# Attention's transposes as pairs of 64x128 blocks on two banks, and the first memory attention's scores on four quarters of the array

## The chip, the cores and the metric

The kernel runs on one core of a Trainium2 chip. The metric is device time in microseconds, the median of three runs. A core has a matrix engine (TensorE, in the profile PE, its weight loads PEld), a vector engine (VectorE, DVE), a scalar engine (ScalarE, ACT), GpSimd (POOL) and a queue engine for transfers (SyncE, SP). TensorE writes only to PSUM, which has eight banks; ScalarE or VectorE copies a result from there to SBUF.

## The reference

Two layers of a trunk over 512 positions of width 1024. Layer 0 mixes with RWKV-7 (12 heads of 64), layer 1 with chunked attention (12 heads, own chunk and 8 chunks before it). Beside each mixer runs a memory attention of four heads over 256 memory tokens. The part that the change touches:

```python
def memory_attention(q_mem, mem_n, w_mem_kv):
    ...
    s = jnp.einsum('bshd,bmhd->bhsm', q, k).astype(jnp.float32) * HEAD_DIM ** -0.5
    p = jax.nn.softmax(s, axis=-1).astype(v.dtype)
    return jnp.einsum('bhsm,bmhd->bshd', p, v).reshape(bsz, seq, D_MEMQ)

def chunk_attention(q, k_pad, v_pad, bias):
    ...
        s = jnp.einsum('bhqd,bhkd->bhqk', qc, kc).astype(jnp.float32) * scale + bias
        ...
        p = jax.nn.softmax(s, axis=-1).astype(vc.dtype)
        return jnp.einsum('bhqk,bhkd->bhqd', p, vc)

for layer in range(DEPTH):
    mix = rwkv7_time_mix(...) or chunk_attention(...)
    mo = memory_attention(q_mem, mem_n, w_mem_kv[layer])
    x = x + jnp.concatenate([mix, mo], axis=-1) @ w_out[layer]
    x = x + conv_glu(rms_norm(x, ln2[layer]), ...)
```

## The kernel before

The program is one stream of instructions for each engine, written by Python generators. `weave` takes several generators, each with a cost, and always continues the one that has done the least share of its own cost; a `yield n` says that about n ns of TensorE work were written. So the costs of the generators set the order in which TensorE sees the work of different stages. Each engine runs its own stream in order and waits at semaphores. The weights of the dense projections come in as f32, are split into a high and a low part (`whi`, `wlo`) and are multiplied in three products (`dense`, lines 241, 242 and 245), always as 128x128 weights with 512 moving columns.

Heads come in pairs, one on partitions 0 to 63, the other on 64 to 127 (`HS[0]`, `HS[1]`). An attention computes its scores with queries on the partitions, does a softmax along the row (a maximum on VectorE, the exponential with its sum on ScalarE, a reciprocal and a scaling on VectorE), transposes the probabilities on TensorE in blocks of 128x128 against the constant `ident`, copies them from PSUM with ScalarE, and multiplies them by the values.

`mem_attention` does this for the memory tokens. `rows` is scores and softmax for one head and two halves `q2` of the positions, `turn` the transposes (line 360) and copies (line 363) of a head, two banks one after the other, and `values` the product with the values (line 370) for both heads `hh` of a pair `f`. It is used twice. In layer 0 (`mA`) the scores are plain f32 matmuls of 64 rows (`score_a`, line 1590), and the generator is woven with `back` for the fifth head pair, `front` and `back` for the sixth, and `out_ahead`, the first products of the output projection. `back` turns RWKV's chunk products into outputs: it begins with small products (lines 1410, 1418, 1424, 1434, 1445, 1453, 1462) and ends with a recurrence of eight steps (lines 1467, 1472 on TensorE, 1468 on VectorE). In layer 1 (`memB`) the scores are split products of 128 rows.

`attention(i, T)` is the chunked attention of head pair `i`. For each quarter `qt` of the positions and each head, `rows` (lines 1788 and 1789, then 1793 to 1797) computes `qt + 1` blocks of probabilities, and `turn` transposes them (line 1803) three row steps later (`LAG`) and copies them (line 1805) into `ptT`. Line 1817 multiplies all four quarters by the values. Six of these generators and `memB` form one chain, woven with the projections of queries, keys and values. Attention has six PSUM banks for the small products (`pss`), the stage of layer 0 four.

Lines 1300 to 1326 in `front` already use the array in parts: line 1314 transposes 64x128 blocks of the two heads in turn into two banks, and lines 1324 and 1326 multiply 64x64 weights on all four quarters.

## Time and profile before

| | |
|---|---|
| median of three runs | 1292.26 us (1291.12 to 1293.33) |
| profiled execution, span from the first to the last instruction | 1292.6 us; the page gives no other time of it |
| TensorE, matmuls | 1260.9 us busy, 10420 records |
| VectorE | 1031.7 us busy |
| ScalarE | 846.4 us busy |
| transposes of the chunked attention (line 1803) | 120, 21.1 us busy, between 759.8 and 910.5 us |
| transposes of the second memory attention (line 360) | 32, 5.1 us busy, between 803.7 and 823.1 us |
| first memory attention, first to last score or transpose | 310.6 to 345.2 us |

The page lists for every engine the time in which it was busy. A matmul in plain f32 leaves two records in the trace, a transpose and a matmul of split operands one. Matmuls overlap: one is counted from its start to the end of its tail, so what one costs is seen from the distance to the start of the next. A shape such as "64*128 64x64" reads: weights on 64 rows and 128 columns of the array, 64 rows by 64 moving columns. A row of the timeline gives the start, the length of the merged row, the engine, the line, and what was written from what.

### The profile page before, as it was taken

Reading aid. Unit: us, or ns where it says so; the run is one execution under the profiler, and the core shown is the slowest. Engines: PE = TensorE matmul, PEld = TensorE weight load, DVE = VectorE, ACT = ScalarE, POOL = GpSimd, SP = SyncE. Lnnn points to the kernel's source line nnn. Section 1 sums busy time; section 2 is a strip of 40 time slices with the busy share of each in tenths; the row PEclk is TensorE's granted clock in tenths of the full one; section 3 lists DMA queues with packets and bytes.
Section 4 is the critical chain, followed back from the end, with each engine's and each line's share of the span. In section 5 each row is a group of like instructions: output and inputs, shape, how many; then the busy total and the mean of one; then the engine's idle time right before and its main releaser. Section 6 shows DMA issues by size and latency. Waiting matters only on the chain.

```text
span 1292.6 us, 26432 instructions
## 1 busy us (share of the span) xinstructions
PE 1260.9 (98%) x10420; PEld 1083.1 (84%) x10420; DVE 1031.7 (80%) x1956; ACT 846.4 (65%) x1398; POOL 152.7 (12%) x182
## 2 busy tenths in 40 slices
PE   9999999999999999999999999999999999999997
PEld 7887777777789999998888878787789999998886
DVE  7867677765688999998876876658889999998684
ACT  6566767856476777776554676757757777765662
POOL 1000000000001222320220000000002222211200
PEclk9999999999999999999999999999999999999999
DMA  5364444453055988996984322234429989978951
GB/s 204 110 174 106 100 96 89 92 109 96 30 166 126 212 198 198 206 208 172 274 185 122 118 87 82 76 104 123 130 61 212 197 193 211 208 161 262 233 149 66
DMA packets 95581, 192.14 MB, mean 149 GB/s; under 512 B 22112, under 2 KB 30432, under 8 KB 95456
## 3 DMA queue, kind: packets, MB, share of 16 engines
q1 hardware_dynamic: 68592, 129.14, 31.9%
q0 software_dynamic: 26864, 61.31, 27.3%
q8 instruction: 82, 1.34, 0.4%
q14 instruction: 43, 0.35, 0.1%
HBM read 174.20 MB, written 6.29 MB: 140 GB/s over the span
## 4 chain that ended last, share of the span: by engine, by line
PE 62%; DVE 15%; ACT 8%; DMA 8%; issue 6%; SPq 0%; POOL 0%; ACTq 0%; DVEq 0%; POOLq 0%
PE psf L434 8%; PE psf L698 7%; PE psd L245 6%; PE psd L241 5%; PE psd L242 5%; DMA wlv<-in_ffn_in_dram 4%; PE psf L436 4%; PE psf L703 4%; PE psd L698 3%; ACT whi L499 2%; DMA wraw<-in_ffn_in_dram 2%; PE psd L703 2%; DVE raw L486 1%; PE pss L1817 1%; DVE wlo L504 1%
## 5 line engine op out<-in xcount | busy, mean ns | idle before, releaser
L499 ACT CAST whi<-raw 128x1024 fp32r<-128x1024 f32 (+1 forms) x168 | 153.3, 942 | 62.3 <-PE psf L434 29.5
L434 PE MATMUL psf<-th,whi 128*128 128x256 f32 x672 | 161.4, 278 | 2.5 <-ACT tmp L553 1.9
L434 PE MATMUL psf<-tl,whi 128*128 128x256 f32 x672 | 161.1, 276 | 0.0
L195 ACT CAST whi<-wraw 128x1024 fp32r<-128x1024 f32 x84 | 87.6, 1048 | 78.3 <-PE psd L242 37.4
L434 PEld LDWEIGHTS psf<-th,whi 128*128 128x128 f32 x672 | 125.8, 188 | 3.9 <-ACT tmp L553 2.9
L434 PEld LDWEIGHTS psf<-tl,whi 128*128 128x128 f32 x672 | 126.0, 188 | 0.0
L504 DVE TENSOR_TENSOR wlo<-raw,whi 128x1024 fp32r<-128x1024 f32 (+1 forms) x108 | 109.3, 1012 | 9.1 <-ACT whi L499 8.9
L241 PE MATMUL psd<-r1h,whi 128*128 128x512 f32 x264 | 107.4, 408 | 0.0
L242 PE MATMUL psd<-r1l,whi 128*128 128x512 f32 x264 | 105.0, 398 | 0.0
L203 DVE TENSOR_TENSOR wlo<-wraw,whi 128x1024 fp32r<-128x1024 f32 x65 | 79.2, 1219 | 22.3 <-ACT whi L195 20.4
L688 ACT CAST whi<-raw 128x1024 fp32r<-128x1024 f32 (+1 forms) x52 | 49.6, 954 | 59.9 <-PE psf L698 33.1
L689 DVE TENSOR_TENSOR wlo<-raw,whi 128x1024 fp32r<-128x1024 f32 (+1 forms) x52 | 56.5, 1097 | 38.9 <-ACT whi L688 31.5
L436 PE MATMUL psf<-th,wlo 128*128 128x256 f32 x504 | 78.0, 276 | 0.0
L245 PE MATMUL psd<-r1h,wlo 128*128 128x512 f32 x264 | 74.3, 403 | 0.6 <-DMA wlo<-in_ffn_in_dram 0.4
L471 POOL DMA_DIRECT2D wlv<-in_ffn_in_dram x40 | 60.7, 1516 | 59.5 <-DVE tmp L572 59.1
L436 PEld LDWEIGHTS psf<-th,wlo 128*128 128x128 f32 x504 | 66.8, 188 | 0.0
L434 PE MATMUL psf<-r2h,whi 128*128 128x256 f32 x252 | 60.9, 278 | 0.7 <-ACT whi L499 0.7
L434 PE MATMUL psf<-r1h,whi 128*128 128x256 f32 x252 | 60.7, 277 | 0.7 <-ACT whi L499 0.7
L434 PE MATMUL psf<-r2l,whi 128*128 128x256 f32 x252 | 60.7, 277 | 0.0
L434 PE MATMUL psf<-r1l,whi 128*128 128x256 f32 x252 | 60.6, 277 | 0.0
L241 PEld LDWEIGHTS psd<-r1h,whi 128*128 128x128 f32 x264 | 49.6, 188 | 12.0 <-issue 2.1
L525 ACT ACTIVATE tmp<-tmp,vec 128x512 f32<-128x512 f32 x44 | 36.0, 817 | 33.3 <-DVE tmp L512 33.3
(611 smaller groups left out, 3576.8 us busy)
## 6 DMA issues: line engine op xcount, KB each, us to landing
raw<-in_ffn_in_dram SPq DMA_DIRECT2D x42, 512.0 KB, 5.2
raw<-in_ffn_in_dram SPq DMA_DIRECT2D x84, 256.0 KB, 5.5
wlv<-in_ffn_in_dram POOLq DMA_DIRECT2D x40, 512.0 KB, 8.6
raw<-in_ffn_out_dram SPq DMA_DIRECT2D x30, 512.0 KB, 6.2
raw<-in_ffn_out_dram POOLq DMA_DIRECT2D x24, 512.0 KB, 8.4
wraw<-in_wA_dram SPq DMA_DIRECT2D x20, 512.0 KB, 4.1
wraw<-in_w_out_dram SPq DMA_DIRECT2D x16, 512.0 KB, 4.1
wraw<-in_ffn_outp_dram SPq DMA_DIRECT2D x16, 512.0 KB, 4.5
```

The costliest lines, as they stand in the source:

```text
L195: high = lambda: pin(SC.copy(hi[:, :n], raw))
L203: pin(V.tensor_tensor(lo[:, :n], raw, hi[:, :n], op=ALU.subtract))
L241: PE.matmul(ps, wh[:, j * P:(j + 1) * P], ah, start=start and n == 0, stop=False)
L242: dense_at[0] = PE.matmul(ps, wh[:, j * P:(j + 1) * P], al, start=False, stop=False)
L245: dense_at[0] = PE.matmul(ps, wl[:, j * P:(j + 1) * P], act(k)[0], start=False, stop=stop and n == len(ks) - 1)
L434: PE.matmul(ps, wh[:, o + k * P:o + k * P + P], x[k][n], start=k == n == 0, stop=False)
L436: PE.matmul(ps, wl[:, ol + k * P:ol + k * P + P], x[k][0], start=False, stop=k == 3)
L471: GP.dma_start(self.low[:].rearrange("p (a s) -> p a s", a=2), self.second, accum_op=ALU.add)
L499: keep(SC.copy(hi[:, :n], self.pair(what) if n > S else self.raw[:, what]))
L504: keep(V.tensor_tensor(lo[:, :n], self.pair(what) if n > S else self.raw[:, what], hi[:, :n], op=ALU.subtract))
L698: PE.matmul(ps[:], a[:, k0 + i, ts], hi[:, i * S:i * S + S], start=bool(first) and (first is True or t in first) and a is act[0] and i == ...
L703: PE.matmul(ps[:], act[0][:, k0 + i, ts], lo[:, i * S:i * S + S], start=False, stop=bool(last) and t in last and i == n - 1)
```

## The change

It does four things.

1. `turned` replaces each transpose of a 128x128 block by two of its halves, 64 rows by 128 columns each, against the 64x64 identity `i64`. Rows 0 to 63 go to one bank, rows 64 to 127 to another, 64 columns each. So a `turn` holds two banks at once, and each bank has every second group of 64 positions.
2. In the chunked attention `turn` takes both heads of a quarter, after `rows` of both heads of the quarter behind it; the transposes of the heads are separated by a yield, and four copies follow, by head and bank, where there were two of double width. The cost of a block falls from 0.85 x 128 = 109 to 68.
3. In `mem_attention`, `turn` has two copies by bank in layer 1 (of the same 512 elements), and four of 256 in layer 0.
4. In layer 0 the scores of both heads are written together, each as two matmuls of 64x64 weights, in the order of `QUADS` over the four quarters of the array, and both heads go through the softmax half by half. The order is now all scores and softmaxes of a pair, then the transposes of both its heads. The costs given to `weave` fall (860 to 450, 430 to 270).

```diff
+    def turned(ps, at, src, of):
+        for i in range(2):
+            PE.transpose(ps[i][:, at:at + 64], src[i * 64:i * 64 + 64, of:of + P], C("i64")[i * 64:i * 64 + 64])
...
+        def scores(f, hhs, q2):
+            ps = {hh: ps_s() for hh in hhs}
+            for qq in range(2):
+                score({hh: ps[hh][:, qq * 256:(qq + 1) * 256] for hh in hhs}, f,
+                      slice((q2 * 2 + qq) * P, (q2 * 2 + qq + 1) * P))
+            return ps
...
         def turn(f, hh):
+            ps = [ps_s() for _ in range(2)]
             for kt in range(2):
-                ps = ps_s()
                 for qt in range(4):
-                    o = (qt % 2) * 256 + kt * P
-                    PE.transpose(ps[:, qt * P:(qt + 1) * P], prs[f, hh, qt // 2][:, o:o + P], C("ident"))
-                yield 430
-                t_ = pts[f, hh, kt] = pt_tile(f, hh, kt)
-                SC.copy(t_, ps[:])
+                    turned(ps, (kt * 4 + qt) * 64, prs[f, hh, qt // 2], (qt % 2) * 256 + kt * P)
+                yield 270
+            ts = [pt_tile(f, hh, kt) for kt in range(2)]
+            for kt in range(2):
+                pts[f, hh, kt] = ts[kt]
+            for i in range(2):
+                pt_copy(f, hh, i, ps[i][:].rearrange("p (k q c) -> p k q c", k=2, c=64))
...
+        if l == 0:
+            for f in range(2):
+                yield from rows(f, (0, 1))
+                if f:
                     yield from values(0)
-        yield from turn(1, 1)
+                yield from turn(f, 0)
+                yield from turn(f, 1)
...
+    QUADS = ((0, 0), (1, 1), (0, 1), (1, 0))
...
-    def score_a(ps, f, hh, qc):
-        PE.matmul(ps, qmA[f][HS[hh], qc], kmT0[HS[hh], f], start=True, stop=True)
+    def score_a(ps, f, qc):
+        for hh, n in QUADS:
+            PE.matmul(ps[hh][HS[n]], qmA[f][HS[hh], qc.start + n * 64:qc.start + n * 64 + 64], kmT0[HS[hh], f], start=True, stop=True)
+
+    def pt_copy_a(f, hh, i, half):
+        for kt in range(2):
+            SC.copy(ptA[hh * 2 + kt].rearrange("p (q c) -> p q c", c=P)[:, :, i * 64:i * 64 + 64], half[:, kt])
...
-            def turn(hh, qt):
-                n = (qt + 1) * P
-                pst_ = ps_s()
-                for kt in range(qt + 1):
-                    PE.transpose(pst_[:, kt * P:(kt + 1) * P], sbs[hh, qt][:, kt * P:(kt + 1) * P], C("ident"))
-                yield n * 0.85
-                SC.copy(pts[hh][:, 0:qt + 1, qt * P:(qt + 1) * P], pst_[:, :n].rearrange("p (a b) -> p a b", b=P))
...
+            def turn(qt):
+                n = qt + 1
+                ps = [ps_s() for _ in range(2)]
+                for hh in range(2):
+                    for kt in range(n):
+                        turned(ps, (hh * n + kt) * 64, sbs[hh, qt], kt * P)
+                    yield n * 68
+                for hh in range(2):
+                    for i in range(2):
+                        SC.copy(pts[hh][:, 0:n, qt * P + i * 64:qt * P + i * 64 + 64],
+                                ps[i][:, hh * n * 64:(hh + 1) * n * 64].rearrange("p (k c) -> p k c", c=64))
+
+            for qt in range(4):
+                yield from rows(0, qt)
+                yield from rows(1, qt)
+                if qt:
+                    yield from turn(qt - 1)
+            yield from turn(3)
```

The first place is TensorE's stream in the chunked attention, the last two turns of head pair 0 among a dense projection (L241, L242), up to the product with the values. A row gives line, operation, written tile and read tiles, the size of what is written, and how many follow. Before:

```order
L241 MATMUL psd<-r2h,whi 128x512
L242 MATMUL psd<-r2l,whi 128x512
L1803 MATMUL pss<-cst,sb 128x128 x4
L241 MATMUL psd<-r2h,whi 128x512
L242 MATMUL psd<-r2l,whi 128x512
L241 MATMUL psd<-r2h,whi 128x512
L242 MATMUL psd<-r2l,whi 128x512
L1803 MATMUL pss<-cst,sb 128x128 x4
L241 MATMUL psd<-r2h,whi 128x512
L242 MATMUL psd<-r2l,whi 128x512
L241 MATMUL psd<-r2h,whi 128x512
L1817 MATMUL pss<-ptT,vS 64x512 x2
```

And the same place now, where L333 is the transpose in `turned` and L1848 the product with the values:

```order
L333 MATMUL pss<-cst,sb 128x64 x8
L241 MATMUL psd<-r2h,whi 128x512
L242 MATMUL psd<-r2l,whi 128x512
L333 MATMUL pss<-cst,sb 128x64 x8
L241 MATMUL psd<-r2h,whi 128x512
L242 MATMUL psd<-r2l,whi 128x512
L241 MATMUL psd<-r2h,whi 128x512
L242 MATMUL psd<-r2l,whi 128x512
L241 MATMUL psd<-r2h,whi 128x512
L1848 MATMUL pss<-ptT,vS 64x512 x2
```

Four blocks have become eight halves, and between the two heads still stand two dense matmuls.

The second place is TensorE's stream at the start of the first memory attention: scores (L1590 before, L1614 now), the recurrence of the fifth head pair (L1467 and L1472, now L1490 and L1495) and `back` of the sixth, which begins with L1410 (now L1433). Before:

```order
L1590 MATMUL pss<-kmT_87,kn 128x256 x4
L1467 MATMUL psl<-W,MQ 64x64 x2
L1472 MATMUL psl<-MQ,W 64x64 x2
L1590 MATMUL pss<-kmT_87,kn 128x256 x2
L1467 MATMUL psl<-W,MQ 64x64 x2
L1410 MATMUL pss<-AR,ML 32x32 x16
L1472 MATMUL psl<-MQ,W 64x64 x2
L1418 MATMUL pss<-VT,ML 64x64 x16
```

Now:

```order
L1614 MATMUL pss<-kmT_87,kn 64x256 x8
L1490 MATMUL psl<-W,MQ 64x64 x2
L1495 MATMUL psl<-MQ,W 64x64 x2
L1614 MATMUL pss<-kmT_87,kn 64x256 x8
L1490 MATMUL psl<-W,MQ 64x64 x2
L1495 MATMUL psl<-MQ,W 64x64 x2
L1490 MATMUL psl<-W,MQ 64x64 x2
L1495 MATMUL psl<-MQ,W 64x64 x2
L333 MATMUL pss<-cst,krv 128x64 x4
```

All scores of the first pair `f` now stand ahead of its transposes, and `back` of the sixth head pair is no longer among them.

The third place is where the transposes of that pair end (`krv` holds the probabilities of head 0, `a` and `Ei` those of head 1). Before, on TensorE, they follow `back`'s last small product, L1462:

```order
L1462 MATMUL psd<-ML,VT 64x64 x16
L1467 MATMUL psl<-W,MQ 64x64 x2
L1472 MATMUL psl<-MQ,W 64x64 x2
L1467 MATMUL psd<-AR,KB 64x64 x2
L1472 MATMUL psd<-KB,AR 64x64 x2
L360 MATMUL pss<-cst,krv 128x128 x4
```

Now `back`'s first one, L1433, follows them:

```order
L333 MATMUL pss<-cst,krv 128x64 x10
L333 MATMUL pss<-cst,Ei 128x64 x2
L1495 MATMUL psl<-MQ,W 64x64
L333 MATMUL pss<-cst,Ei 128x64 x2
L333 MATMUL pss<-cst,a 128x64 x4
L333 MATMUL pss<-cst,Ei 128x64 x4
L1433 MATMUL pss<-AR,ML 32x32 x16
L1441 MATMUL pss<-VT,ML 64x64 x16
L1447 MATMUL pss<-Tt_94,AR 32x32 x16
L1614 MATMUL pss<-kmT_87,kh 64x256 x8
```

The transposes of the first pair and the small products of the sixth head pair have changed places.

More of the change, by code (lines that the diff above doesn't have):

```diff
@@ L373, in values @@
             dst(f, pso)
-        for f in range(2):
-            for hh in range(2):
-                yield from rows(f, hh)
-                n = f * 2 + hh
-                if n > 0:
-                    yield from turn((n - 1) // 2, (n - 1) % 2)
-                if n == 2:
-                    yield from values(0)
-        yield from turn(1, 1)
+        if l == 0:
+            for f in range(2):
+                yield from rows(f, (0, 1))
+                if f:
+                    yield from values(0)
+                yield from turn(f, 0)
+                yield from turn(f, 1)
+        else:
+            for f in range(2):
+                for hh in range(2):
+                    yield from rows(f, (hh,))
+                    n = f * 2 + hh
+                    if n > 0:
+                        yield from turn((n - 1) // 2, (n - 1) % 2)
+                    if n == 2:
+                        yield from values(0)
+            yield from turn(1, 1)
         yield from values(1)
     def mem_cost(score):
-        return 2 * (2 * (2 * score + 2 * 430) + 1720)
+        return 2 * (2 * (2 * score + 2 * 270) + 1720)
     def out_ahead(l, act, order, n, pre):
@@ L1851, in pt_tile, with pt_copy @@
             return ptB[f][:, hh * 2 + kt]
+        def pt_copy(f, hh, i, half):
+            to = ptB[f][:, hh * 2:hh * 2 + 2].rearrange("p k (q c) -> p k q c", c=P)
+            SC.copy(to[:, :, :, i * 64:i * 64 + 64], half)
         Tm = [{}, {}]
```

40 lines of the change are left out of this document (18 added, 22 removed).

## The prediction

> **What bounds the kernel now.** I read the page first, then the chain of waits, then the busy time by stretch for the two places that the change touches, and last the timeline of TensorE, instruction by instruction.
>
> ```profile
> span 1292.6 us, 26432 instructions
> PE 1260.9 (98%) x10420; PEld 1083.1 (84%) x10420; DVE 1031.7 (80%) x1956; ACT 846.4 (65%) x1398; POOL 152.7 (12%) x182
> PE 62%; DVE 15%; ACT 8%; DMA 8%; issue 6%; SPq 0%; POOL 0%; ACTq 0%; DVEq 0%; POOLq 0%
> ```
>
> TensorE is busy almost all of the span, and 62% of the chain that ended last is its work. The two places, by stretch (columns: stretch, length, busy PE, PEld, DVE, ACT, POOL, granted clock, DMA share, GB/s):
>
> ```profile
> 310.00:325.00 15.00, 14.81 (x284) 12.18 (x283) 11.90 (x31) 9.59 (x31) 0.00 (x0) 1.00 0.13 39
> 755.00:835.00 80.00, 78.44 (x453) 61.56 (x452) 54.98 (x149) 56.81 (x142) 0.58 (x4) 1.00 0.27 86
> 835.00:915.00 80.00, 78.35 (x444) 60.04 (x442) 53.79 (x152) 52.81 (x124) 1.00 (x5) 1.00 0.32 96
> ```
>
> The first row is the first memory attention, woven into RWKV's last head pairs. The other two are the chunked attention with the second memory attention inside, woven with dense projections: of 160.0 us TensorE is idle 3.2, while VectorE and ScalarE are busy some 54 each in 80. So in both places what TensorE's queue gains or loses goes nearly one to one into the time. Because matmuls overlap their neighbours, I price them by distance from start to start, not by duration.
>
> **The change part by part: transposes in the chunked attention and the second memory attention.** A group of four old transposes in the dense stream (columns: start, length of the merged row, what):
>
> ```profile
> 862.45 0.39 PE L242 MATMUL psd<-r2l,whi 128*128 128x512 f32 x1
> 862.68 0.60 PE L1803 MATMUL pss<-cst,sb 128*128 128x128 f32 x4
> 863.03 0.48 PE L241 MATMUL psd<-r2h,whi 128*128 128x512 f32 x1
> 863.35 0.40 PE L242 MATMUL psd<-r2l,whi 128*128 128x512 f32 x1
> ```
>
> A dense matmul takes 0.23 (862.45 to 862.68). The four take 0.35 to L241's start and L241 takes 0.32 instead of 0.23, so four cost 0.44: 0.11 each, and nothing for going in and out, since weights are 128*128 on both sides.
>
> The new form, 64 rows by 128 columns in pairs on two banks, stands already in the kernel as L1314, and L1300 is a plain matmul on the same 64*128 shape between dense ones:
>
> ```profile
> 95.22 0.61 PE L245 MATMUL psd<-r1h,wlo 128*128 128x512 f32 x2
> 95.76 0.71 PE L1314 MATMUL pss<-cst,KB 64*128 64x64 f32 x16
> 96.40 0.83 PE L1082 MATMUL pss<-cst,tmp 128*128 128x2 f32 x6
> 85.76 0.39 PE L241 MATMUL psd<-r1h,whi 128*128 128x512 f32 x1
> 85.99 0.39 PE L242 MATMUL psd<-r1l,whi 128*128 128x512 f32 x1
> 86.31 1.16 PE L1300 MATMUL pss<-AR,KB 64*128 64x128 f32 x16
> 87.40 0.50 PE L241 MATMUL psd<-r1h,whi 128*128 128x512 f32 x1
> 87.74 0.39 PE L242 MATMUL psd<-r1l,whi 128*128 128x512 f32 x1
> ```
>
> L1314's eight pairs take 0.64 from start to start. Its last row, with its 0.22 of tail, ends at 96.47, so the last pair starts near 96.25 and seven steps fill 0.49. The first of them holds part of the entry; one pair in the middle takes about 0.062. So a whole block costs 0.062 instead of 0.109, a gain of 0.047. But going in and out costs. Entering, the dense matmul ahead takes 0.32 instead of 0.23 (85.99 to 86.31; for L245, 0.54 for two instead of 0.46): 0.09. Inside, L1314's 0.64 is 0.14 more than eight times 0.062. Leaving, the dense matmul behind takes 0.34 instead of 0.23 (87.40 to 87.74): 0.10. Together 0.33 for each run of pairs among 128*128 work. One run of m blocks changes by 0.33 - 0.047 m: it needs seven blocks to pay.
>
> The runs have fewer. The number of blocks, and how long TensorE waited ahead of them:
>
> ```profile
> L1803 PE MATMUL pss<-cst,sb 128*128 128x128 f32 x120 | 21.1, 276 | 1.6 <-DVE st L1796 1.1 <-DVE sb L1797 0.2
> L360 PE MATMUL pss<-cst,sb 128*128 128x128 f32 x32 | 5.1, 277 | 0.0
> L1803 PEld LDWEIGHTS pss<-cst,sb 128*128 128x128 f32 x120 | 14.8, 140 | 8.9 <-DVE sb L1797 1.4 <-ACT ptT L1805 1.2 <-PE psd L241 1.1
> ```
>
> That is 152 blocks. In the new order of TensorE they stand in 53 runs, of 1 to 8 blocks; the yield between the two heads in turn lets two dense matmuls in between, as the order rows in the section on the change show. So 53 x 0.33 = 17.5 lost and 152 x 0.047 = 7.1 won: +10.4 us. Cover: where TensorE waited for the softmax anyway, the way in is hidden. Its matmul side idled 1.6 us ahead of L1803 (first row); its load side 8.9 (third row), but most of that lies under a running dense matmul. I take 1.6, with 0 and 8.9 as ends.
>
> ScalarE now empties the pairs with copies of half the columns, twice as many:
>
> ```profile
> L1805 ACT COPY ptT<-pss 128x512 f32<-128x512 f32 x12 | 6.8, 582 | 1.2 <-PE pss L1803 1.2
> L1805 ACT COPY ptT<-pss 128x384 f32<-128x384 f32 x12 | 5.5, 470 | 0.1
> L1805 ACT COPY ptT<-pss 128x256 f32<-128x256 f32 x12 | 4.3, 362 | 2.0 <-PE pss L1803 2.0
> L1805 ACT COPY ptT<-pss 128x128 f32<-128x128 f32 x12 | 2.9, 250 | 0.2 <-PE pss L1803 0.2
> L1817 PEld LDWEIGHTS pss<-ptT,vS 128*64 128x64 f32 x96 | 9.0, 136 | 10.1 <-ACT ptT L1805 5.1 <-issue 2.9 <-ACT ks L1862 0.2
> ```
>
> One step in columns of 128 costs 0.11, so 64 columns cost about 0.195 and 192 about 0.306. A head pair had 2 x (0.250 + 0.362 + 0.470 + 0.582) = 3.33 us and gets 4 x (0.195 + 0.250 + 0.306 + 0.362) = 4.45: 1.1 more, 6.7 for six pairs, on an engine that is busy 55 in 80. Most of it hides behind dense matmuls. What shows is the end of each pair: values (L1817) needs the last turn whole. Before, one copy of 0.58 stood behind the last transpose, now four of 0.36, 1.45 together: 0.87 later, with dense matmuls between. L1817 already waited 5.1 for these copies on the load side. I take 0.2 a pair, 1.2 in all; ends 0 and 6 x 0.87 = 5.2. The softmax of head 1 gets one row step less before its transposes; I price that at nothing because head 0's run and two dense matmuls cover it, and without this cover it is the 0.7 or so of a longer wait in a few turns. The second memory attention has as many copies as before, of the same 512 elements.
>
> This place: 10.4 - 1.6 + 1.2 = +10.0 us.
>
> **First memory attention.** Its scores before, in 64*64 surroundings, and four quarters of the array at work (L1324 and L1326):
>
> ```profile
> 327.18 0.28 PE L1472 MATMUL psd<-KB,AR 64*64 64x64 f32 x4
> 327.39 1.13 PE L1590 MATMUL pss<-kmT,kh 64*128 64x256 f32 x4
> 328.45 0.33 PE L1467 MATMUL psd<-AR,KB 64*64 64x64 f32 x4
> 91.36 0.22 PE L1324 MATMUL pss<-cst,AR 64*64 64x64 f32 x2
> 91.38 0.23 PE L1326 MATMUL pss<-cst,v 64*64 64x64 f32 x2
> 91.42 0.23 PE L1324 MATMUL pss<-cst,AR 64*64 64x64 f32 x2
> 91.43 0.23 PE L1326 MATMUL pss<-cst,v 64*64 64x64 f32 x2
> ```
>
> A matmul in f32 leaves two records, so the group at 327.39 is two matmuls, 1.06 until the next start. Without the way in and out it is four records of 0.216; eight such groups are some 8.3 us (the first two adjoin). Four quarters start their four records every 0.058 (91.36, 91.42), which for 64 columns is what one quarter needs alone; at 256 columns I take 0.216 a round. New: both heads, two query tiles, four rounds, 0.87 a group without a change of shape beside L1467, four groups, 3.7 with one entry: -4.6. Its 32 blocks of transposes give 32 x 0.047 = -1.5, less some 0.3 where the order puts the same bank in a row. Runs among other shapes are as many as before there (counted in TensorE's order up to the first feed-forward: 226 changes of shape, against 227): nothing.
>
> Against that stands the order. Before, TensorE did back's products of the last head pair (L1410 at 314.27 to L1462) while the first softmaxes ran, and the transposes came behind. Now back's first product stands behind all transposes of f = 0, and these wait for four softmaxes in a row:
>
> ```profile
> L343 DVE TENSOR_REDUCE mst<-pss 128x2 f32<-128x512 f32 x16 | 11.0, 685 | 11.7 <-PE pss L1870 8.9 <-PE pss L1590 2.7
> L347 ACT ACTIVATE krv<-pss,mst 128x256 f32<-128x256 f32 x8 | 3.7, 477 | 2.1 <-DVE mst L343 2.1
> L349 DVE RECIPROCAL mst<-mst 128x2 f32<-128x2 f32 x16 | 2.5, 159 | 2.0 <-ACT sb L347 1.6 <-ACT Ei L347 0.3
> L352 DVE TENSOR_SCALAR krv<-krv,mst 128x256 f32<-128x256 f32 x8 | 2.4, 347 | 0.0
> 314.27 0.69 PE L1410 MATMUL pss<-AR,ML 32*32 32x32 f32 x32
> ```
>
> VectorE needs 0.685 + 0.159 + 2 x 0.347 = 1.54 for each of the four, 6.2 us; beside it TensorE has the second scores (0.9) and a few steps of the other pair's recurrence. I take 4.5 us of new waiting over both f, and 0.3 for the copies that now stand ahead of back's X on ScalarE (sixteen of 0.36 for eight of 0.59). Sum: -4.6 - 1.2 + 4.5 + 0.3 = -1.0; ends -5.8 (no wait) and +3.3 (6.2 and 2.9 of copies in the way).
>
> **Sum.** 1292.6 - 1.0 + 10.0 = 1301.6 for an execution like the profiled one; the median of the runs, 1292.26, is 0.4 below its span: 1301 us.
>
> **A rule weighed.** The Trainium skill, "TensorEngine Tiling (Array Packing)", Key Properties, says that changing the tiling mode, not just the tile, drains TensorE. It speaks against this change; by it each run of pairs pays twice, which agrees with L1300's 0.32 and 0.34. It has no figure, so the sum by it is the sum above.
>
> **Rivals.** (1) The change of shape is free in the new places, since the softmax waits hide it or it overlaps: -7.1 and -1.0, 1284 us, faster. For it speaks only that L1803 has waits ahead; against it the rows at 86.31 and 95.76. 0.06. It decides below some 0.13 a run (7.1 / 53). (2) Waits cover 8.9 of it and the first memory attention loses nothing: 10.4 - 8.9 - 5.8 = -4.3, 1288 us. For it speaks PEld's 8.9; against it TensorE's 3.2 idle in 160. 0.08. (3) ScalarE's copies show in full ahead of values: +5.2 in place of 1.2, or 1305, and up to 1308 if all 6.7 shows. For it L1817's 5.1, against it ScalarE's 55 in 80. 0.12. (4) The first memory attention's waits are whole, +3.3: 1305.6. 0.09. (5) A pair of half blocks takes as long as a whole block, because loading 128 columns sets the pace: 184 x 0.047 = 8.6 more, 1310. L1314's sixteen in 0.64 speak against it. 0.03. The Trainium skill, "TensorE: Matmul & The Clock Gate", section "LDWEIGHTS (loading the stationary operand)", states this rule: the load goes by columns, not by rows. By it two loads in one block would give no gain; the trace disagrees, sixteen loads of 128 columns start in 0.64 us.
>
> **How the numbers follow.** The forecast, with its own range 1297 to 1305, gets 0.62. Below 1294 lie (1) and (2), 0.14; above 1308 about 0.05; so 1294 to 1308. 0.2% (2.6 us) is about what a measurement here can tell from no change. Faster: (1) and five of eight of (2), 0.11. Same: the rest of (2) and the forecast's low tail, 0.07. Slower: 0.82.
>
> **What would show it.** Right: L333's pairs step by about 0.06; the dense matmul ahead of each run takes 0.32 and the one behind 0.34; the stretch of chunked attention is about 10 us longer with no more idle; L1614's sixteen records take 0.9; TensorE idles ahead of L333 for VectorE near 313 to 318, and back's first 32*32 product starts some 4 us later. Wrong: dense matmuls around L333 at 0.23, or waits ahead of the old transposes that shrink by what the runs cost.

## The result, and the profile after

| | before | after |
|---|---|---|
| median of the runs | 1292.61 us (4 runs, 1291.12 to 1293.33) | 1308.53 us (4 runs, 1306.08 to 1312.33) |
| ratio | | 1.0128, 95% interval 1.0107 to 1.0150 |
| span of the profiled execution | 1292.6 us | 1304.3 us, time 1306.08 |
| mean granted clock of TensorE | 0.997 | 0.994 |

The change makes the kernel 15.9 us slower; forecast was 8.7 slower. The sign and the larger of the two terms were right, the other term had the wrong sign. Wherever both are on record, the time of a run is 1.8 us above its span. So the profiled execution of before, whose own time is not given, took some 1294.4 us (an estimate), 1.8 above its median; that of after lies 2.4 below its own. Hence the traces differ by 11.7 us at their ends where the medians differ by 15.9.

The page of after, its head, engine line and chain:

```profile
span 1304.3 us, 26943 instructions
PE 1268.5 (97%) x10636; PEld 1080.1 (83%) x10636; DVE 1033.2 (79%) x1956; ACT 851.0 (65%) x1454; POOL 152.9 (12%) x182
PE 63%; DVE 15%; ACT 8%; DMA 7%; issue 7%; SPq 0%; POOL 0%; ACTq 0%; DVEq 0%; POOLq 0%
```

TensorE is counted busy for 7.6 us more, work at a lowered clock included, and idle for 4.1 more; its share fell from 98% to 97%. By stretch, as before (length, busy PE, PEld, DVE, ACT, POOL, granted clock, DMA share, GB/s):

```profile
310.00:325.00 15.00, 12.23 (x198) 9.77 (x196) 8.69 (x25) 8.22 (x30) 0.00 (x0) 0.65 0.11 37
755.00:835.00 80.00, 78.56 (x517) 57.37 (x516) 48.46 (x128) 52.34 (x142) 0.84 (x4) 1.00 0.24 80
835.00:915.00 80.00, 79.14 (x478) 57.90 (x476) 53.84 (x140) 52.19 (x139) 0.84 (x5) 1.00 0.32 103
915.00:929.00 14.00, 13.54 (x92) 8.84 (x91) 8.05 (x34) 9.39 (x34) 0.00 (x0) 1.00 0.01 1
```

The chunked attention (three last rows) is as full as before, only longer. The first memory attention shows what before did not: TensorE idles 2.8 of 15 us, and the clock granted to it is 0.65 instead of 1.00.

**The second stretch** runs from its first score to its last product with the values. Timeline rows of before, then of after:

```profile
748.26 0.33 PE L1788 MATMUL pss<-ks,qs 128*128 128x128 f32 x1 [0.18 <-ACT ks L1747]
910.68 3.11 PE L1817 MATMUL pss<-ptT,vS 128*64 128x512 f32 x16
```

```profile
752.52 0.33 PE L1816 MATMUL pss<-ks,qs 128*128 128x128 f32 x1
925.08 2.83 PE L1848 MATMUL pss<-ptT,vS 128*64 128x512 f32 x16
```

162.4 us became 172.6, up to the start of that last product: +10.1, forecast +10.0. A run of pairs in it:

```profile
772.12 0.39 PE L241 MATMUL psd<-r2h,whi 128*128 128x512 f32 x1
772.34 0.40 PE L242 MATMUL psd<-r2l,whi 128*128 128x512 f32 x1
772.67 0.46 PE L333 MATMUL pss<-cst,sb 64*128 64x64 f32 x8
773.06 0.50 PE L241 MATMUL psd<-r2h,whi 128*128 128x512 f32 x1
773.39 0.40 PE L242 MATMUL psd<-r2l,whi 128*128 128x512 f32 x1
```

The dense matmul ahead takes 0.33 (772.34 to 772.67) instead of 0.23, the one behind 0.33 (773.06 to 773.39), and four pairs 0.39 where four times 0.062 would be 0.25. That is 0.10 + 0.14 + 0.10 = 0.34 for going in and out, against 0.33 in the prediction.

**The first memory attention.** TensorE's timeline in after:

```profile
309.06 1.09 PE L1614 MATMUL pss<-kmT,kn 64*64 64x256 f32 x16
...
311.91 0.33 PE L1490 MATMUL psl<-W,MQ 64*64 64x64 f32 x4 [0.67 <-DVE W L1491]
...
313.30 0.33 PE L1490 MATMUL psl<-W,MQ 64*64 64x64 f32 x4 [0.94 <-DVE W L1491]
...
314.90 0.57 PE L333 MATMUL pss<-cst,krv 64*128 64x64 f32 x4 [1.16 <-DVE krv L364]
...
320.39 1.06 PE L1433 MATMUL pss<-AR,ML 32*32 32x32 f32 x32
321.38 1.97 PE L1441 MATMUL pss<-VT,ML 64*64 64x64 f32 x32
...
324.27 1.99 PE L1614 MATMUL pss<-kmT,kh 64*64 64x256 f32 x16
```

The new scores are as fast as forecast: sixteen records take 0.9 from start to start, and the row's length is 1.09. Then TensorE waits three times for VectorE, 2.77 us in all. `back`'s first product stands at 320.39, before at 314.27. And the scores of the second pair, the same sixteen records, take 1.99: the clock has halved. Rows of one us around its edges:

```profile
313.00:314.00 1.00, 0.45 (x8) 0.31 (x8) 1.00 (x5) 1.00 (x7) 0.00 (x0) 1.00 0.00 0
314.00:315.00 1.00, 0.10 (x1) 0.13 (x2) 1.00 (x4) 1.00 (x6) 0.00 (x0) 0.79 0.00 0
...
327.00:328.00 1.00, 1.00 (x14) 1.00 (x12) 0.60 (x1) 0.91 (x4) 0.00 (x0) 0.50 0.00 0
328.00:329.00 1.00, 1.00 (x20) 1.00 (x18) 0.78 (x3) 0.99 (x5) 0.00 (x0) 0.88 0.00 0
```

The rows between show 0.50 and those around 1.00, nothing else. So a mean of 0.79 means that the clock fell at 314.58, and 0.88 that it rose at 328.24: 13.7 us at half the clock, in which TensorE was busy almost throughout.

### The profile page after: what moved, and what is told of

It reads as the page before. It is cut to its first block, busy times and chain, and to the rows that moved or that the text cites. A ratio compares the mean times of both kernels' runs of the same rounds, so it can differ in the third digit from the quotient of the medians.

```text
span 1304.3 us, 26943 instructions
## 1 busy us (share of the span) xinstructions
PE 1268.5 (97%) x10636; PEld 1080.1 (83%) x10636; DVE 1033.2 (79%) x1956; ACT 851.0 (65%) x1454; POOL 152.9 (12%) x182
## 4 chain that ended last, share of the span: by engine, by line
PE 63%; DVE 15%; ACT 8%; DMA 7%; issue 7%; SPq 0%; POOL 0%; ACTq 0%; DVEq 0%; POOLq 0%
PE psf L456 7%; PE psf L720 7%; PE psd L241 6%; PE psd L245 5%; PE psd L242 5%; DMA wlv<-in_ffn_in_dram 4%; PE psf L458 4%; PE psf L725 4%; PE psd L720 3%; ACT whi L521 2%; PE pss L333 2%; PE psd L725 2%; DVE raw L508 1%; PE pss L1848 1%; DVE wlo L526 1%
## 5 line engine op out<-in xcount | busy, mean ns | idle before, releaser
L241 PE MATMUL psd<-r1h,whi 128*128 128x512 f32 x264 | 107.6, 409 | 0.0
L242 PE MATMUL psd<-r1l,whi 128*128 128x512 f32 x264 | 105.3, 399 | 0.0
L241 PEld LDWEIGHTS psd<-r1h,whi 128*128 128x128 f32 x264 | 49.5, 188 | 12.0 <-issue 1.5
L245 PEld LDWEIGHTS psd<-r1h,wlo 128*128 128x128 f32 x264 | 47.5, 188 | 12.9 <-issue 1.3
```

The lines of the kernel that those rows point to most:

```text
L241: PE.matmul(ps, wh[:, j * P:(j + 1) * P], ah, start=start and n == 0, stop=False)
L242: dense_at[0] = PE.matmul(ps, wh[:, j * P:(j + 1) * P], al, start=False, stop=False)
L245: dense_at[0] = PE.matmul(ps, wl[:, j * P:(j + 1) * P], act(k)[0], start=False, stop=stop and n == len(ks) - 1)
```

## The experiments

"A" is the first memory attention, "B" the second stretch. All times are medians; each batch has its own runs of before (1292.69, 1291.24, 1292.39, 1292.22 and 1292.09 for e1 to e4, e5 to e8, e9 to e12, e13 to e15 and e16 to e18).

### Which part costs what: e1 and e2

e1 leaves A as before; e2 leaves B as before (`mem_attention_old` and the old `turn` are those of before).

```diff
 e1, against after
-    mA = mem_attention(0, score_a, 450, dst_mem, lambda hh, q2: prA[q2] if hh else kt_("krv", bufs=2),
+    mA = mem_attention_old(0, score_a, 860, dst_mem, lambda hh, q2: prA[q2] if hh else kt_("krv", bufs=2),
 e2, against after
-        memB = mem_attention(1, score_b, 430, dst_memb,
+        memB = mem_attention_old(1, score_b, 430, dst_memb,
...
-            def turn(qt):
+            def turn(hh, qt):
...
```

> The first memory attention as before, the rest of the change kept (64x128 pairs in the chunked attention and the second memory attention). Theory W (the whole miss lies in the first memory attention, where TensorE idles near 311 to 315 us and its granted clock then halves): the stretch of attention is 10 us longer, as forecast, and nothing else moves: 1302 to 1303 us. Rival S (the first memory attention gives -1 as forecast, and the pairs cost more than the forecast's 0.33 a run): 1308 us or more.

> Only the first memory attention is changed; all transposes of layer 1 are whole 128x128 blocks as before. Theory W: idle TensorE near 311 to 315 us and a clock of 0.5 for some 12 us behind it; the start of the feed-forward comes 4 to 5 us later: 1296 to 1299 us. Rival S: 1291 us, no spell of low clock.

e1: 1302.74, +10.05 (ratio 1.0076, 1.0063 to 1.0088). e2: 1299.90, +7.2 (1.0059, 1.0047 to 1.0071). Together 17.3 for the 15.9 measured. So B costs what was forecast, and A, forecast at -1.0, costs 7. e2 shows the same picture as after (310 to 315, then 315 to 330):

```profile
310.00:315.00 5.00, 2.23 (x48) 1.43 (x39) 5.00 (x12) 2.51 (x12) 0.00 (x0) 1.00 0.00 0
315.00:330.00 15.00, 14.91 (x224) 12.31 (x226) 6.45 (x21) 9.03 (x31) 0.00 (x0) 0.66 0.14 38
```

### What the loss of B is made of: e4, e12, e8

e4 keeps B's new order and its four copies, but transposes whole 128x128 blocks, one bank for each head; A and the second memory attention are as before. e12 adds to e4 one pair of half blocks ahead of each of the 24 turns, over which the whole blocks then write.

```diff
 e4, against e1 (second memory attention as before, too)
-                        turned(ps, (hh * n + kt) * 64, sbs[hh, qt], kt * P)
+                        PE.transpose(ps[hh][:, kt * P:kt * P + P], sbs[hh, qt][:, kt * P:kt * P + P], C("ident"))
 e12, against e4
+                turned(ps, 0, sbs[0, qt], 0)
```

> Both memory attentions as before. The chunked attention keeps the change's order (both heads of a quarter in one turn) and its four copies of half the columns, but transposes whole 128x128 blocks, one bank for each head. Theory W (in this stretch the changes of shape are the cost): the 53 x 0.33 go, and the forecast's 1.2 for copies and order is left: 1292 to 1295 us. Rival C (the copies on ScalarE and the order are the cost): 1299 us or more.

> e4 (whole blocks in the new order with the new copies, 1292.4) with one pair of half blocks added ahead of each of the 24 turns of the chunked attention; the whole blocks then write over it. It adds 24 runs of pairs and 24 pairs. Theory W (0.33 for each run, 0.06 for a pair): 24 x 0.39 = 9.4, 1301.8 (1299 to 1304). Rival (what the change lost goes with the half blocks themselves, 10 us on 152 blocks, 0.066 each): 1.6 to 3, 1294 to 1295.5.

e4: 1292.44, -0.25 (1.0002, 0.9993 to 1.0012). No cost of the copies and the order is seen. The interval, -0.9 to +1.6 us, still allows the 1.2 that were forecast, but not the 7 of rival C. e12: 1301.09, 8.7 above e4, 0.36 for each added run with its pair; forecast were 0.39 for each, and 1.6 to 3 in all by the rival. One of them in the trace of e12:

```profile
764.62 0.40 PE L242 MATMUL psd<-r2l,whi 128*128 128x512 f32 x1
764.95 0.27 PE L333 MATMUL pss<-cst,sb 64*128 64x64 f32 x2
765.15 0.66 PE L1883 MATMUL pss<-cst,sb 128*128 128x128 f32 x4
765.57 0.47 PE L241 MATMUL psd<-r2h,whi 128*128 128x512 f32 x1
```

The dense matmul ahead takes 0.33 instead of 0.23, the pair 0.20, the four whole blocks 0.42 instead of the 0.35 they took before: 0.37 more. But from the first score to the last product with the values the profiled run of e12 takes 168.8 us and that of e4 163.2: there the 24 add only 5.5, or 0.23 each, in part because some stand where TensorE waited anyway (from 748 to 913 it idles 1.8 us instead of 3.1). The rest of the 8.7 came behind this stretch, most of it in one wait of 3.1 us for ScalarE between 955 and 980, and is not explained by the pairs. So the rival falls by the 5.5 too, but that the medians give nearly the forecast 0.39 is partly luck.

e8 was meant to lower the number of runs from 53 to 37 by joining both heads' pairs, with the dense matmuls queued behind them (`behind_turn` is an order edge to the last transpose of a turn).

```diff
                 for hh in range(2):
                     for kt in range(n):
                         turned(ps, (hh * n + kt) * 64, sbs[hh, qt], kt * P)
-                    yield n * 68
+                yield 2 * n * 68
...
-            PE.matmul(ps, wh[:, j * P:(j + 1) * P], ah, start=start and n == 0, stop=False)
+            with behind_turn():
+                PE.matmul(ps, wh[:, j * P:(j + 1) * P], ah, start=start and n == 0, stop=False)
...
```

> The second stretch as changed, the first memory attention as before; the pairs of both heads of a turn adjoin, with the dense matmuls that stood between them behind them: 37 runs of pairs in TensorE's order instead of 53, the same 152 blocks and the same copies. Theory W (a fixed price for each run): 37 x 0.33 = 12.2 lost and 7.1 won, +5.1: 1297.4 (1296 to 1299), 5.3 below the 1302.7 with 53 runs. Rival (the loss goes with the number of half blocks, or comes from waits for the softmax): no gain or a loss by longer waits, 1301 to 1304.

Both theories missed: 1341.88 (1.0375, 1.0351 to 1.0398). By stretch:

```profile
755.00:835.00 80.00, 72.31 (x470) 52.19 (x469) 47.78 (x128) 50.39 (x141) 0.58 (x4) 1.00 0.25 80
835.00:915.00 80.00, 68.81 (x384) 52.23 (x382) 45.61 (x123) 44.34 (x120) 0.68 (x4) 0.87 0.29 89
915.00:955.00 40.00, 33.08 (x169) 21.21 (x169) 16.69 (x50) 17.58 (x53) 0.20 (x1) 0.71 0.19 56
```

TensorE idles 25.8 us in 200, because the dense matmuls that now queue behind a turn had covered its wait for the softmax. And the clock falls to 0.87 and 0.71. It says nothing on the price of a run, but that these dense matmuls are the cover, and that the clock is lower here too, beside the waits.

### Why A loses: order, doubled scores, VectorE (e3, e11, e5, e6, e7)

All five leave B as before. e3 puts a pause in A's generator ahead of the transposes, so that `back`'s products come ahead of them. e11 keeps the new scores and order but transposes whole blocks. e5 and e6 issue every matmul of the scores twice, in e2 and in e3. e7 is e3 with the splits of earlier heads' results written behind the first softmaxes (`with_splits` runs `flush_mix` between them and the pause).

```diff
 e3, against e2
+                yield 0, 6000
                 yield from turn(f, 0)
 e11, against e2: turn(f, hh) of before in place of the new one
 e5 against e2, e6 against e3
-        for hh, n in QUADS:
+        for hh, n in QUADS + QUADS:
 e7, against e3
-           (told(chain(q_mem(lambda f: A["wA"][18 + f], hact, qmA), flush_mix(), mA), "mem"),
+           (told(chain(q_mem(lambda f: A["wA"][18 + f], hact, qmA), with_splits(mA)), "mem"),
```

> As the one with the first memory attention alone, but with a pause of 6000 ns told to the weave between softmax and transposes, so that back's small products of the sixth head pair stand ahead of the transposes in TensorE's order again. Theory W: no long idle, no low clock, and the gain of scores and transposes shows: 1286 to 1289 us. Rival (the four quarters or the pairs of transposes are themselves dear in this place): no better than the run before by more than 1 us, 1296 to 1299.

> Of the change only the first memory attention's scores on four quarters, with both heads' softmax together and the transposes of a pair behind them, but as whole 128x128 blocks, one bank after the other, and two copies of 512; the rest as before. If the loss of the first memory attention comes from its scores and their order: 1299 to 1301, as with half blocks (1299.9). If half blocks (64x128) and their copies cost a part of it: 1295 to 1298.

> The first memory attention as changed (second stretch as before), with every matmul of its new scores issued twice into the same place; the result is the same, TensorE does about 4 x 0.9 = 3.7 us more. Theory S (starved: the new scores end before VectorE can take them, TensorE idles, and the idle is followed by a granted clock of 0.5): the second copy fills most of the 2.8 us that TensorE idled between 310 and 315, the clock stays near 1.00 between 315 and 330, and the kernel with more work is faster than the one with single scores: 1294 to 1296 against 1299.9. Rival O (only the order costs: transposes ahead of back's products, the last recurrence late): the waits stay and the work is added: 1300 to 1304.

> The kernel with the pause (back's products ahead of the transposes; single scores: 1298.9, granted clock 0.52 and 0.80 between 315 and 325), with every matmul of the new scores issued twice. Theory S: the 1.8 us idle between 310 and 315 is filled, the clock stays at 1.00, back's first product starts at 314 to 315, and the time is 1293 to 1295.5, although TensorE does 3.7 us more than in the single one. Rival O: clock or no clock, the late end of the softmaxes between 345 and 355 is what costs: 1298 to 1302.

> The kernel with the pause and single scores; the four splits of the earlier head pairs' results (VectorE, 0.63 each) are written behind the first softmaxes instead of ahead of them, and in VectorE's order two of the four come after the first reductions. Theory S with VectorE as what starves: the first step of the recurrence and the first reductions come about 1.2 us earlier, TensorE idles 0.5 to 1 instead of 1.8 between 310 and 315, the clock stays above 0.9: 1294 to 1296.5 against 1298.9. If VectorE's splits are not what it waits for: 1298 to 1300, with the same idle.

e3: 1298.93 (1.0055, 1.0036 to 1.0074), far from the 1286 to 1289 expected. `back`'s first product is at 314.0 again, so the order was not the main thing. TensorE still waits, and the clock still falls:

```profile
310.00:315.00 5.00, 3.23 (x88) 2.28 (x82) 5.00 (x12) 2.52 (x10) 0.00 (x0) 1.00 0.00 0
315.00:330.00 15.00, 14.40 (x280) 13.21 (x280) 7.10 (x23) 9.40 (x31) 0.00 (x0) 0.77 0.13 38
```

e11: 1298.90 (1.0046, 1.0031 to 1.0062). The scores and their order alone bring the loss. e5: 1303.29 (1.0085, 1.0070 to 1.0100) and e6: 1300.61 (1.0068, 1.0054 to 1.0083): theory S missed in this form. e5 shows why:

```profile
310.00:315.00 5.00, 4.98 (x79) 3.30 (x78) 4.45 (x8) 2.08 (x4) 0.00 (x0) 1.00 0.02 5
315.00:330.00 15.00, 11.27 (x182) 8.88 (x186) 6.09 (x20) 8.40 (x29) 0.00 (x0) 0.66 0.12 37
```

The added work fills 310 to 315, but the softmax that TensorE waits for comes behind the scores, so the wait moves behind 315, with 3.7 us of work added. Work covers a wait only if it is independent of what is waited for and stands between the two.

e7: 1296.27 (1.0034, 1.0024 to 1.0045), within what was expected of VectorE's order. Each against its own runs of before, though, e7 loses 5.0 and e3 6.2, and the two intervals overlap. And the clock, expected above 0.9, fell all the same. The 3.4 us ahead of that, and rows of one us at its edges:

```profile
311.80:315.20 3.40, 2.57 (x82) 2.07 (x80) 3.40 (x12) 3.24 (x14) 0.00 (x0) 1.00 0.00 0
```

```profile
315.00:316.00 1.00, 0.85 (x27) 0.74 (x29) 1.00 (x4) 0.98 (x3) 0.00 (x0) 0.64 0.00 0
...
322.00:323.00 1.00, 1.00 (x22) 1.00 (x20) 0.03 (x2) 0.51 (x2) 0.00 (x0) 0.94 0.51 205
```

In the 3.4 us ahead of the fall TensorE counted as busy for 2.57, with small products, and never waited longer than 0.41 at a time.

### Work that holds the clock: e9 and e10

Products that nobody reads stand ahead of each step of the fifth pair's recurrence in e7: sixteen of 64x64 (e9), or four of 128x128 by 64 columns (e10).

```diff
 e9, against e7
             if c and i == NPAIR - 2:
+                for at in (0, 7) * 4:
+                    for h in range(2):
+                        PE.matmul(psc[HS[h], at], cst[HS[h], 0:64], cst[HS[h], 0:64], start=True, stop=True)
 e10, against e7
+                for at in (0, 7) * 2:
+                    PE.matmul(psc[:, at], cst[:, 0:P], cst[:, 0:64], start=True, stop=True)
```

> The kernel with pause and splits behind (e7: 1296.3, TensorE idle 1.75 in 310 to 317 in short pieces, granted clock 0.53 and 0.79 in 315 to 325), with sixteen products of 64x64 on a constant, which nobody reads, ahead of each step of the fifth pair's recurrence, where TensorE waits for VectorE; they add work and leave the result as it is. Theory C (the halved clock is what costs, some 6.4 us at half speed): the clock stays at 1.00, the last recurrence ends about 3 us earlier, 1293 (1291 to 1294.5), although TensorE does about 3 us more. If work on two quarters of the array doesn't hold the clock, or the clock costs nothing: 1296 to 1299.

> As e9, but the work that nobody reads is four products of 128x128 weights by 64 columns ahead of each step, so the whole array runs, at the price of a change of shape each time (7 x 0.33). Theory C: the clock stays at 1.00 here too, 1293 to 1296 (what the changes of shape aren't covered by waits comes on top). If the clock doesn't matter: 1298 to 1301.

e9: 1300.28 (1.0056, 1.0044 to 1.0068), e10: 1297.57 (1.0042, 1.0030 to 1.0054). The stretch from 315 to 330 in e9, then in e10:

```profile
315.00:330.00 15.00, 13.79 (x416) 13.13 (x415) 8.26 (x25) 7.26 (x25) 0.00 (x0) 1.00 0.13 39
```

```profile
315.00:330.00 15.00, 14.47 (x306) 13.01 (x299) 8.76 (x26) 6.96 (x25) 0.00 (x0) 1.00 0.14 38
```

The clock stays at 1.00 in both, as expected, but there is no gain: the fill takes 1.0 us a step, 7 us in all, more than the waits. Yet e10 is 5.2 above its own runs of before, and e7, without the fill, is 5.0 above its own. So in e10 some 7 us of added work cost next to nothing: the covered waits and the full clock are worth about as much together. What the clock is worth by itself was not separated from this.

### Real work in the waits: e13, e14, e16, with the control e15

The 24 dense matmuls that project the queries of the second pair stood ahead of the first scores. e13 puts them, and the splits, behind the scores of the first pair; e14 adds a pause of 3 us ahead of the transposes; e16 puts nine steps of them between the two halves' scores. Nothing is added. e15 is the kernel before, with its old scores and whole blocks, and the same new place.

```diff
 e13, against e2
-           (told(chain(q_mem(lambda f: A["wA"][18 + f], hact, qmA), flush_mix(), mA), "mem"),
+           (told(chain(q_mem(lambda f: A["wA"][18 + f], hact, qmA, (0,)), mA), "mem"),
...
                 yield from rows(f, (0, 1))
                 if f:
                     yield from values(0)
+                else:
+                    yield from between()
...
+                       lambda: chain(q_mem(lambda f: A["wA"][18 + f], hact, qmA, (1,)), flush_mix()))
 e14, against e13
+                yield 0, 3000
                 yield from turn(f, 0)
 e16, against e14 (mid is the generator of that projection and the splits)
+                    if q2 and mid:
+                        for _ in range(9):
+                            yield next(mid)
                     pss = scores(f, hhs, q2)
```

> The first memory attention as changed (second stretch as before), with real work in its waits: the projection of the queries of the second pair (24 dense matmuls, 5.5 us) and the splits of the mix come between the first pair's scores and its transposes, instead of ahead of the first scores. No work is added. Theory S (the loss of the first memory attention is TensorE waiting for the softmax, and the halved clock that follows): the granted clock stays at 1.00 from 305 to 330, and the 7.2 us of e2 are gone: 1290 to 1294. If the loss lies elsewhere (transposes ahead of back's products, the last recurrence late): 1296 to 1300.

> As e13, with a pause of 3 us ahead of the transposes, so that back's first products stand ahead of them in TensorE's order. Theory S: clock 1.00, TensorE idles less than 0.5 in 305 to 325, and of the 5 us that the new scores and half blocks save on TensorE some 2 to 4 show: 1288 to 1291, faster than before. If the sixth pair's recurrence sets the end in any case: 1292 to 1294; if the loss lies elsewhere: 1296 or more.

> The kernel before (whole blocks, old scores) with only this new place of the second projection and of the splits. Nothing is saved on TensorE, which had no waits there: 1291 to 1294. If it is the order that wins and not the scores: 1288 to 1290, as e14.

> As e14 (first memory attention as changed, second projection behind the first scores, pause; 1294.5), where TensorE still waited 3.1 us at 300 to 305 for ScalarE to empty the banks of the first scores before the second could be written (all four banks are held), and the clock fell to 0.77. Here the first nine steps of the second projection stand between these two groups of scores, so that real work covers that wait as well. Theory S: no wait over 0.5 us and clock 1.00 from 296 to 330, and the saved TensorE time shows: 1287 to 1290. If the chain of the recurrences sets the end: 1291 to 1293. If waits and clock were not the loss: 1294 and more.

e13: 1298.13 (1.0043, 1.0026 to 1.0060), little of it back: TensorE waits 2.6 us ahead of the second half's scores, and the clock, expected at 1.00, is 0.50 from 305.6 to 309.0. e14: 1294.46 (1.0020, 1.0010 to 1.0031). In e14 (stretches, then its longest wait):

```profile
300.00:305.00 5.00, 1.93 (x13) 0.61 (x10) 1.87 (x7) 3.13 (x11) 0.00 (x0) 0.89 0.75 232
305.00:310.00 5.00, 5.00 (x125) 3.95 (x125) 4.24 (x12) 2.74 (x11) 0.00 (x0) 0.77 0.05 14
```

```profile
PE pss L1672 <- ACT krv L359: 3.1, 1, 3.1
```

Both heads' scores of one half hold two of the four small banks, and `back`'s products the others; the second half's scores wait until ScalarE's exponentials have emptied theirs. Wait and low clock had only moved some 10 us ahead. e16 covers this too:

```profile
300.00:310.00 10.00, 9.27 (x227) 6.83 (x223) 5.62 (x15) 5.54 (x19) 0.00 (x0) 1.00 0.42 129
310.00:315.00 5.00, 5.00 (x103) 3.60 (x103) 3.96 (x10) 4.16 (x13) 0.00 (x0) 1.00 0.00 0
315.00:330.00 15.00, 14.73 (x285) 12.10 (x282) 7.78 (x21) 8.41 (x25) 0.00 (x0) 1.00 0.13 39
```

1290.77 (0.9994, 0.9985 to 1.0002): with the same instructions as e2 in another order, the loss of 7.2 is gone and the clock is 1.00. So the loss was the waits and the clock behind them. But the saved work shows no gain either: the control e15 gives 1290.83 (0.9986, 0.9976 to 0.9997). In the trace of e16 the output projection starts 2.9 us earlier than in before (353.92 against 356.82; 354.88 in e15), and that is lost again in the first feed-forward (the two longest waits of TensorE between 395 and 425 in e16; the first was 0.2 in before):

```profile
PE psf L518 <- ACT tmp L637: 2.1, 1, 2.1
PE psf L520 <- DMA wlv<-in_ffn_in_dram: 1.2, 1, 1.2
```

e15 is the one version whose interval lies below 1: 0.14% faster than before.

### Half blocks in A alone: e17 and e18

```diff
 e17 against before, e18 against e15: the new turn in layer 0 alone
-                    yield from turn((n - 1) // 2, (n - 1) % 2)
+                    yield from (turn if l else turn_half)((n - 1) // 2, (n - 1) % 2)
```

> The kernel before with one part of the change alone: the transposes of the first memory attention (32 blocks) as half blocks, with two banks and four copies of 256 a head; old scores, old order, old second stretch. The prediction's term: -1.2 for the transposes and +0.3 for copies, so 1291.4 (1290.5 to 1292.5). If half blocks lose here as in the second stretch (some 10 runs among other shapes at 0.33): 1294 to 1296. If the four copies delay what stands behind them on ScalarE: 1293 to 1294.

> e15 (old scores, second projection behind the first two heads' scores; 1290.8) with the half blocks of e17 in the first memory attention. If the two add: 1289.5 to 1290. If half blocks cost there: 1292 to 1295.

e17: 1294.99, +2.9 (1.0027, 1.0017 to 1.0036), at granted clocks of 0.997 to 0.999. e18: 1291.36 (1.0001, 0.9988 to 1.0013), 0.5 above e15. The forecast gain of 0.9 is not there; in the order of before half blocks cost some 3 us, in that of e15 nothing that can be told. Why they cost 3 was not followed up: the profiled run of e17 was one of its two fastest, 2.3 below its median.

## Why the prediction was right in B and wrong in A

**Right: the second stretch.** 53 runs at 0.33, 152 blocks at -0.047 and the cover of 1.6 make 8.8; e1 measured 10.05, and the stretch in after is 10.1 longer at the same clock with no more idle time (0.86 + 1.44 in 160 us for 3.2 before). The rows of the runs show the price (0.34). It goes by runs: in the trace of after, runs of one, two, three and four pairs take 0.20, 0.27, 0.33 and 0.39 to the next start, which is 0.14 once and 0.06 a pair. e12 agrees in kind and only roughly in size (0.36 a run by the medians, 0.23 in the stretch itself), and e4 shows that without half blocks nothing is lost. Rivals 1 (free switches), 2 (waits cover all) and 5 (a pair as slow as a block) fall with it. The rule weighed, of the Trainium skill ("TensorEngine Tiling (Array Packing)", Key Properties), says that a change of mode drains TensorE. The traces agree, with 0.34 a run. The term of 1.2 for the copies was not seen (e4: -0.25, at most 1.6 by its interval). So rival 3, 5.2 for them, falls too; by its own terms its upper figure was 1307, not 1308. That 8.8 + 1.2 hit 10.0 so closely is partly luck, within the 1.6 of e1's interval.

**Wrong: the first memory attention, forecast -1.0, measured +7.2 (e2).** The steps in the prediction's order:

- "-4.6" for the scores. The sixteen records take 0.9 as forecast, but the saving is not worth its time. Before, those scores were what TensorE did while VectorE worked; when they end earlier, TensorE waits. This is the step that failed first: work that stands in a wait was priced by its length. e11 has this term and the next but one alone, -4.6 + 4.5 = -0.1, and measured +6.5. e16 against e15 shows the other side: no wait, and no gain.
- "-1.2" for the transposes and "+0.3" for the copies: e17 has +2.9 in their place, e18 about +0.5 over e15.
- "+4.5" for new waiting. The mechanism was right: TensorE idles ahead of L333 for VectorE (2.8 us between 311 and 315), and `back`'s first product comes 6.1 later (4 forecast). What was missing is what came behind the waits, a clock that the prediction left at 1.00: 13.7 us at half the clock. In that time TensorE waited for almost nothing, so the same work at full clock would have taken 6.8 less, an upper bound. Rival 4 (all waits, +3.3) was the right direction and too small for that reason.

After and e2 wait once more at the end of A: the last step of the sixth pair's recurrence is 9.8 us later than in before, and the output projection waits for that pair's result (the first row is of before, the others of after):

```profile
335.78 0.33 PE L1472 MATMUL psd<-KB,AR 64*64 64x64 f32 x4
345.58 0.33 PE L1495 MATMUL psd<-KB,AR 64*64 64x64 f32 x4
360.21 0.50 PE L241 MATMUL psf<-r1h,whi 128*128 128x512 f32 x1 [2.44 <-DVE tmp L1528]
```

What is shown: taking waits and low clock away together (e16) removes the loss. How the two share it can be estimated from the traces. From the first score of A to the first matmul of the output projection before takes 46.2 us (310.65 to 356.82) and after 51.2 (309.06 to 360.21), with six dense matmuls less, 1.4 us, in it. So A costs some 6.4 there. TensorE idles 5.3 us in it instead of 0.2, 5.1 more, and the clock costs at most 6.8. The difference, 5.1 + 6.8 - 6.4 = 5.5, is work that TensorE was spared, near the 5.8 that the prediction had (4.6 and 1.2): it was saved, and waits and clock took more than it. The granted clocks of all runs fit: the mean over e2's six runs is 0.0048 below that over the 17 runs of before beside them (0.9930, 0.9978), which over 1300 us is 6.2 us at most. No run takes away the clock's part alone; e9 and e10 hold the clock only at a price that hides its gain.

**The sum.** With +7.2 for A the same working would have given 1292.3 + 10.0 + 7.2 = 1309.5; measured are 1308.5.

## What to carry to other kernels

Half blocks on 64 rows are cheaper than whole ones, but a run of them among 128x128 work costs about 0.34 us here, so count the runs in TensorE's order, not the blocks. Before shortening work on the busiest engine, ask what it covers: if the next thing in its queue waits for another engine, the time saved is idle time, and in every version here that left such waits in A open (after, e2, e3, e5, e6, e7, e11, e13, e14) the clock fell to half behind them. Cover that helps is independent work between the producer and the wait (e16), not more of the work that the wait hangs on (e5).

## What the runs showed of the hardware that was not expected

The granted clock fell to 0.50 and stayed there for whole multiples of 3.4 us, although TensorE was busy again at once: 13.7 us in after (314.58 to 328.24), 10.2 in e2, e5, e6 and e11, 6.8 in e3 and e7 (315.28 to 322.12 in e7), 3.4 in e13 and e14. The Trainium skill, "TensorE: Matmul & The Clock Gate", "Part 1: The HAM clock gate", describes a gate that passes half of the pulses after an idle window of about 3.4 us and opens after a busy one; the 0.50 and the multiples agree. But one busy window did not always open it again: in after it took four, with TensorE counted busy for 13.3 of the 13.7 us.

TensorE's idle time in the profile does not tell when such a fall comes. In e7 the longest wait in the 3.4 us ahead of the fall was 0.41, with TensorE counted busy for 2.57. In e2 the clock fell a second time, from 340.2 to 343.6, with no idle time in the 3.4 us ahead of it; TensorE was counted busy there with half blocks, 64x64 products and products of two columns:

```profile
335.00:340.00 5.00, 5.00 (x64) 3.42 (x61) 4.23 (x18) 3.26 (x13) 0.00 (x0) 1.00 0.01 3
340.00:345.00 5.00, 5.00 (x20) 1.67 (x19) 1.45 (x8) 1.55 (x6) 0.00 (x0) 0.66 0.00 0
```

In e9, where sixteen unread 64x64 products stood ahead of each step, it held at 1.00 through 3.4 us with TensorE busy for 2.3 (314.60 to 318.01). Nor does the shape of the products decide alone: before ran `back`'s 32x32 and 64x64 products between 314 and 325 at 1.00, with TensorE busy for 14.81 of the 15 us from 310. What does decide is open.
